# Chunk states stored chunk by chunk and advanced by one step per chunk; silu of two gates taken later, in place

## The chip, the cores and the metric

The kernel runs on one core of a Trainium2 chip. The metric is the device time of one execution in microseconds (us); lower is better. The kernel before has a median of 1754.92 us over 3 runs (1752.55 to 1758.75).

## The reference, cut to what matters

The program is two layers of a hybrid network over 512 latent and 256 context positions of width 1024, followed by a second block (window attention, a gated delta rule, cross-attention and a feed-forward part), which the change does not touch. Each of the first two layers has four branches (short convolution, attention, a gated recurrence called HGRN, a Fourier mix). Each branch is multiplied by `silu` of a gate projection. The recurrence, for 4 heads of width 64 and in both directions d:

```python
def step(state, inp):                       # one chunk of positions
    qc, kc, vc, lf = inp
    a = jnp.cumsum(lf, axis=2)
    a_last = a[:, :, -1:, :]
    s_new = jnp.exp(a_last)[:, :, 0, :, None] * state + jnp.einsum(
        "bhsk,bhsv->bhkv", kc * jnp.exp(a_last - a), vc)
    inter = jnp.einsum("bhtk,bhkv->bhtv", qc * jnp.exp(a), state)
    ...
    return s_new, inter + intra
```

The context chunks come first, then the latent chunks start from the context's last state. `mix_stream` and `hybrid_layer` give the gates: `silu(az)` multiplies the attention output, `silu(hz)` the HGRN output, `silu(cz)` the convolution, `silu(fz)` the Fourier mix.

## The kernel before, in words

Activations lie transposed (channels on the 128 partitions, positions along the free axis), each fp32 matrix is held as a rounded high part and a low part, and every product of the large projections is three matmuls (`mm3`, L187 to L191). Weights come by DMA into `raw`, and `split` (L193) makes the high part `wh` on ScalarE (L194) and the low part `wl` on VectorE or GpSimd (L195).

A layer (`layer`, L547) runs `hgrn` first, then attention with the Fourier and convolution work, then the output projection. `hgrn` (L737) does two rounds, j = 0 and 1, each for two of the four heads (two heads of 64 channels fill 128 partitions). A round computes the decay gates of both directions (Sigmoid, L753 and L754, then Ln, L783), in round 0 also the queries (Silu, L772) and the values `ivt`, and then drives the generator `hgrn_pair` (L807), with projections of gate columns put between its steps:

- round 0: `gate(y[4:6])` (HGRN gates) stands ahead of the pair; `gate(y[2:4])` (attention gates) follows the pair's first step; `gate(y[6:8])` (Fourier gates) follows the second.
- round 1: `gate(y[0:2])` (convolution gates) follows the first step.

`gate` (L993) runs two column blocks of the projection and evicts each from PSUM with a Silu at L998: 128x512 for the latent and, in layer 0 only, 128x256 for the context. `y[2]`, `y[3]`, `y[6]` and `y[7]` are read again only in the attention stage (L1112, L1174).

`hgrn_pair` makes four parts (`hgrn_part`, L834), in the order forward context, forward latent, backward context, backward latent. Chunks are 32 positions: 8 context chunks, 16 latent chunks, 24 states for each direction. A part's first half makes the decayed keys and queries with Exp on ScalarE (L853 to L887) and multiplications on VectorE. Its second half transposes the keys on TensorE (L894), evicts them (`KT`, L896), multiplies keys by values for each chunk (L906, into one double PSUM bank `sc` and two banks `sm`), and evicts these products to the state tile `S` with three copies on ScalarE: L912 for the first two chunks of each 128 positions, and L914 twice for the third and the fourth. The scores (L923) take the same two `sm` banks again, so each of the two score banks needs its L914 to be over. In layer 1 the context parts make no scores. Then VectorE masks and sums the scores (L931 to L939).

The state tile is `S[128, 64, 24]`: value column first, chunk innermost, so that neighbouring value columns of one chunk are 96 bytes apart. After each latent part `hgrn_scan` (L941) makes the recurrence over 24 chunks for all 64 columns with one instruction on VectorE, after spreading the 24 decays to a tile `de` of 1536 columns:

```python
nc.vector.memset(dec[:, 0:1], 0.0)
nc.vector.tensor_copy(de, dec[:, None, :].to_broadcast([128, 64, 24]))
nc.vector.tensor_tensor_scan(S2, de..., S2, 0.0, ALU.mult, ALU.add)
```

`hgrn_out` (L950) then accumulates the outputs: L976 multiplies scores by values (32x64 operands) and queries by the state before each chunk (64x64 operand, `Ss[d][..., :, c - 1]`, read with the 96 byte step). ScalarE squares the sums (L983), and L832 multiplies the normalized result into `y[4 + j]`.

Program order is not engine order. The framework that builds the program plans each engine's order ahead of time: it starts what its own estimate says is ready, the earlier in the program first where several are. Each engine then runs its queue strictly in that planned order, and waits on semaphores. Table loads of ScalarE stand in the queue wherever the next function needs another table than the last.

Of the kernel before, what the change touches and what calls it, by code (L numbers as in the profile page):

```python
# [9 lines left out]
F32 = mybir.dt.float32  # L10
# [3 lines left out]
AF = mybir.ActivationFunctionType  # L14
ALU = mybir.AluOpType
# [5 lines left out]
S = 512  # L21
CTX = 256
T = S + CTX
# [124 lines left out]
class K:  # L148
# [588 lines left out]
    def hgrn(self, l, w_in, need, hp):  # L737
        nc = self.nc
        segs = ((0, 512), (512, 256))
        nt = 6 if need else 4  # L740
        self.hgmask = hp.tile([128, 192], I32, tag="hgmask", name="hgmask", bufs=1)
        nc.scalar.dma_start(self.hgmask, self.I["c_hgmask"])
        self.scanmask = hp.tile([128, 512], F32, tag="scanmask", name="scanmask", bufs=1)
        nc.scalar.dma_start(self.scanmask, self.I["c_scanmask"])
        ivt = hp.tile([128, 6, 256], F32, tag="ivt", name="ivt", bufs=1)
        qs = [None, None]
        for j in range(2):
            u = self.first if l == j == 0 else self.units.take()
            kk = [hp.tile([128, T], F32, tag="kk", name="kk") for _ in range(2)]
            lf = [hp.tile([128, T], F32, tag="lf", name="lf") for _ in range(2)]  # L750

            def evac(d, p, c0, n):
                nc.scalar.activation(kk[d][:, c0:c0 + n], p, AF.Sigmoid, scale=-1.0)  # L753
                nc.scalar.activation(lf[d][:, c0:c0 + n], p, AF.Sigmoid)  # L754

            for d in range(2):
                evac(d, self.cp_gemm(u[d], need_lat=False, tag=("mm" if j else "sm"))[1], 512, 256)
            if j == 0:
                ps = self.lat_gemm(u, ("mm", "mm"))
                self.units.more()  # L760
                for d, p in enumerate(ps):
                    evac(d, p, 0, 512)
            else:
                for d in range(2):
                    evac(d, self.cp_gemm(u[d], need_ctx=False, more=d == 1)[0], 0, 512)
            self.fill()
            if j == 0:
                u = self.units.take()
                for jj in range(2):
                    pl, pc = self.cp_gemm(u[jj], need_ctx=need, more=jj == 1)  # L770
                    q = hp.tile([128, T], F32, tag="q", name="q")
                    nc.scalar.activation(q[:, 0:512], pl, AF.Silu)  # L772
                    if need:
                        nc.scalar.activation(q[:, 512:768], pc, AF.Silu)
                    qs[jj] = q
                self.fill()
                for i, ps in self.tp_panel():
                    nc.scalar.activation(ivt[:, i, :], ps, AF.Copy)
                    if i in (1, 4):
                        self.fill()  # L780
            for d in range(2):
                sc_, bi = self.lscale[:, l, d, j:j + 1], self.lbias[:, l, d, j:j + 1]
                nc.scalar.activation(lf[d], lf[d], AF.Ln, scale=sc_, bias=bi)  # L783
                if l:
                    nc.vector.tensor_scalar(kk[d], kk[d], sc_, None, ALU.mult)
            self.dbg(f"lf{l}{j}0", lf[0]); self.dbg(f"lf{l}{j}1", lf[1])
            if j == 0:
                self.gate(self.y[4:6], need)
            steps = self.hgrn_pair(l, j, kk, lf, qs[j], ivt, need, nt, hp)
            next(steps)  # L790
            if j == 0:
                self.gate(self.y[2:4], need)
                next(steps)
                self.gate(self.y[6:8], need)
                next(steps, None)
            else:
                self.gate(self.y[0:2], need)
                next(steps)
                u = self.units.take()
                for jj in range(2):  # L800
                    for p, (c0, n) in zip(self.cp_gemm(u[jj], need_ctx=need, more=jj == 1), self.segs(need)):
                        ys = self.y[jj][:, c0:c0 + n]
                        nc.vector.tensor_tensor(ys, ys, p, ALU.mult)
                self.fill()
                next(steps, None)

    def hgrn_pair(self, l, j, kk, lf, q, ivt, need, nt, hp):  # L807

        nc = self.nc
        sc = hp.tile([128, 6, 2, 32], F32, tag="sc", name="sc", bufs=1)  # L810
        Ss = [hp.tile([128, 64, 24], F32, tag="S", name="S") for _ in range(2)]
        decs = [hp.tile([128, 24], F32, tag="dec", name="dec") for _ in range(2)]
        parts = [self.hgrn_part(d, c0, n, kk[d], lf[d], q, ivt, need or c0 == 0, j, Ss[d], decs[d], sc, hp)
                 for d in range(2) for c0, n in ((512, 256), (0, 512))]

        next(parts[0])
        for n in range(4):
            if n < 3:
                next(parts[n + 1])
            next(parts[n], None)  # L820
            if n % 2:
                self.hgrn_scan(Ss[n // 2], decs[n // 2], hp)
        yield
        on = self.hgrn_out(lf, Ss, sc, ivt, nt, j, hp)
        yield
        y = self.y[4 + j]
        for (i0, n) in ((0, 4), (4, 2))[:2 if need else 1]:
            tr = self.psum("tr", [128, 128 * n])
            for ii in range(n):
                nc.tensor.transpose(tr[:, 128 * ii:128 * ii + 128], on[:, i0 + ii].rearrange("p h v -> p (h v)"), self.ident)  # L830
            ys = y[:, 128 * i0:128 * (i0 + n)]
            nc.vector.scalar_tensor_tensor(ys, tr, self.col[:, 40 + 2 * l + j:41 + 2 * l + j], ys, ALU.mult, ALU.mult)  # L832

    def hgrn_part(self, d, c0, n, kk, lf, q, ivt, out, j, St, dec, sc, hp):  # L834

        nc = self.nc
        sl = slice(c0, c0 + n)
        nch = n // 32
        ntile = n // 128
        a = hp.tile([128, 512], F32, tag="a", name="a", bufs=1)[:, :n]  # L840
# [8 lines left out]
        o0 = 0 if c0 else 8  # L849
# [51 lines left out]
        for ii in range(ntile):  # L901
            i = c0 // 128 + ii
            for A in range(4):
                rs = slice(32 * A, 32 * A + 32)
                for p in range(2):
                    nc.tensor.matmul(ups[A][64 * p:64 * p + 64, ii], KT[rs, 128 * ii + 64 * p:128 * ii + 64 * p + 64],  # L906
                                     ivt[rs, i, 128 * j + 64 * p:128 * j + 64 * p + 64], start=True, stop=True)
        sv = St[:, :, o0:o0 + nch]
        if d:
            sv = sv[:, :, ::-1]  # L910
        sv = sv.rearrange("p v (i a) -> p a i v", a=4)
        nc.scalar.activation(sv[:, 0:2], u2[:, :, :64 * ntile].rearrange("p a (i v) -> p a i v", v=64), AF.Copy)  # L912
        for A in (2, 3):
            nc.scalar.activation(sv[:, A], ups[A], AF.Copy)  # L914
# [23 lines left out]
                nc.vector.tensor_reduce(s1, M.rearrange("p i (l t) -> p i t l", l=3), AX.X, ALU.add)  # L938
                nc.vector.tensor_tensor(so, so, s1, ALU.add)  # L939

    def hgrn_scan(self, St, dec, hp):  # L941

        nc = self.nc
        nc.vector.memset(dec[:, 0:1], 0.0)
        de = hp.tile([128, 64, 24], F32, tag="de", name="de", bufs=1)
        nc.vector.tensor_copy(de, dec[:, None, :].to_broadcast([128, 64, 24]))
        S2 = St.rearrange("p v c -> p (v c)")
        nc.vector.tensor_tensor_scan(S2, de.rearrange("p v c -> p (v c)"), S2, 0.0, ALU.mult, ALU.add)

    def hgrn_out(self, Qas, Ss, sc, ivt, nt, j, hp):  # L950

        nc = self.nc
        o = self.psum("sc", [128, 2, 512])
        for i in range(nt):
            todo = {}
            for A in range(4):
                qsl = slice(32 * A, 32 * A + 32)
                for p in range(2):
                    t = [(sc[qsl, i, p, :], ivt[qsl, i, 128 * j + 64 * p:128 * j + 64 * p + 64])]
                    for d in range(2):  # L960
                        if i >= 4:
                            c = 4 * (i - 4) + A
                            c = c if d == 0 else 7 - c
                        else:
                            c = 4 * i + A
                            c = 8 + (c if d == 0 else 15 - c)
                        if c == 0:
                            continue
                        x0 = 128 * i + 32 * A
                        t.append((Qas[d][64 * p:64 * p + 64, x0:x0 + 32], Ss[d][64 * p:64 * p + 64, :, c - 1]))  # L970
                    todo[A, p] = t

            for n_ in range(3):
                for (A, p), t in todo.items():
                    if n_ < len(t):
                        nc.tensor.matmul(o[32 * A:32 * A + 32, p, 64 * i:64 * i + 64], *t[n_], start=(n_ == 0), stop=(n_ == len(t) - 1))  # L976
# [13 lines left out]
    def segs(self, need):  # L990
        return ((0, 512), (512, 256)) if need else ((0, 512),)

    def gate(self, tiles, need):  # L993

        u = self.units.take()
        for j in range(2):
            for p, (c0, n) in zip(self.cp_gemm(u[j], need_ctx=need, more=j == 1), self.segs(need)):
                self.nc.scalar.activation(tiles[j][:, c0:c0 + n], p, AF.Silu)  # L998
        self.fill()

    def attention(self, l, w_in, need, ap):
# [1087 lines left out]
```

## Time and profile before

| | |
|---|---|
| median of 3 runs | 1754.92 us (1752.55 to 1758.75) |
| the profiled execution | 1756.17 us, of which its span is 1754.4 us |
| TensorE matmul busy | 1630.6 us, 93% of the span |
| VectorE busy | 1017.9 us, 58% |
| ScalarE busy | 872.1 us, 50% |
| GpSimd busy | 220.4 us, 13% |
| mean granted TensorE clock | 0.965 of 2.4 GHz |

PE is TensorE's matmul side, PEld its weight load, DVE is VectorE, ACT is ScalarE, POOL is GpSimd. A name such as `S<-sc` is the tile written and the tile read. "L914" is a line of the kernel. An entry in square brackets at the end of a timeline row is how long the engine stood idle ahead of it, and what ended that idle time. Some 30 such rows stand below.

### The profile page before, as it was taken

The page shows a single profiled execution, that of the slowest core. Times are in us where ns is not written, and L with a number is a line of the kernel's source. Part 1 is how long each engine was busy: PE and PEld are TensorE (multiplying, and loading weights), DVE is VectorE, ACT ScalarE, POOL GpSimd, SP SyncE. Part 2 cuts the span into 40 slices and gives each one's busy share as a digit, 9 for nine tenths or more (in the row PEclk, how much of TensorE's full clock was granted, in tenths as well). Part 3 has the DMA queues.
Part 4 walks back from the last instruction along what each step waited for, and adds up shares of the span by engine and source line. Part 5 has one row for each costly group of instructions (what it writes and reads, how often), then busy time and mean ns, then how long its engine had stood idle before and what let it go on. Part 6 is the DMA issues. An engine that isn't in the chain of part 4 may idle for free. (4 is left out here: it accounts for less than half of the span.)

```text
span 1754.4 us, 31468 instructions
## 1 busy us (share of the span) xinstructions
PE 1630.6 (93%) x12731; PEld 1334.6 (76%) x12731; DVE 1017.9 (58%) x2133; ACT 872.1 (50%) x1754; POOL 220.4 (13%) x226
## 2 busy tenths in 40 slices
PE   5998979999999887999999889999999999999998
PEld 3876758877778675879787668777788888888886
DVE  4635473676565546586777896778766633333223
ACT  4844662553467474455556732666555533333222
POOL 2100001101230000110213443002100011111000
PEclk8998989999999898999999997999999999999999
DMA  9231203202454111213764234102724533332431
GB/s 361 104 122 51 96 27 130 98 1 67 166 161 168 51 49 56 96 49 96 265 208 135 73 90 97 37 25 70 230 85 168 181 88 99 99 99 85 156 109 72
DMA packets 162574, 193.86 MB, mean 111 GB/s; under 512 B 15054, under 2 KB 124910, under 8 KB 160252
## 3 DMA queue, kind: packets, MB, share of 16 engines
q1 hardware_dynamic: 156604, 183.37, 32.2%
q10 hardware_dynamic: 5824, 8.47, 1.7%
q8 instruction: 100, 1.64, 0.4%
q14 instruction: 46, 0.38, 0.1%
HBM read 175.28 MB, written 13.66 MB: 108 GB/s over the span
## 5 line engine op out<-in xcount | busy, mean ns | idle before, releaser
L194 ACT ACTIVATE wh<-raw 128x512 fp32r<-128x512 f32 (+1 forms) x458 | 282.3, 628 | 435.6 <-PE mm L190 161.2
L195 DVE TENSOR_TENSOR wl<-raw,wh 128x512 fp32r<-128x512 f32 x416 | 285.1, 699 | 357.7 <-ACT wh L194 344.7
L189 PE MATMUL mm<-xh,wh 128*128 128x512 f32 x520 | 208.4, 401 | 1.4 <-ACT acc L1627 1.0
L191 PE MATMUL mm<-xh,wl 128*128 128x512 f32 x520 | 208.1, 401 | 0.0
L190 PE MATMUL mm<-xl,wh 128*128 128x512 f32 x520 | 207.8, 400 | 0.0
L191 PE MATMUL gl<-xh,wl 128*128 128x512 f32 (+1 forms) x480 | 182.4, 381 | 6.0 <-DVE wl L195 3.9
L189 PE MATMUL gl<-xh,wh 128*128 128x512 f32 (+1 forms) x480 | 181.7, 379 | 3.5 <-ACT y L998 2.5
L190 PE MATMUL gl<-xl,wh 128*128 128x512 f32 (+1 forms) x480 | 180.6, 377 | 0.1
L189 PEld LDWEIGHTS mm<-xh,wh 128*128 128x128 f32 x520 | 100.6, 193 | 23.0 <-ACT acc L1627 1.9
L191 PEld LDWEIGHTS mm<-xh,wl 128*128 128x128 f32 x520 | 100.4, 193 | 20.5
L190 PEld LDWEIGHTS mm<-xl,wh 128*128 128x128 f32 x520 | 100.3, 193 | 20.5
L189 PEld LDWEIGHTS gl<-xh,wh 128*128 128x128 f32 x480 | 93.4, 195 | 22.8 <-issue 3.4
L191 PEld LDWEIGHTS gl<-xh,wl 128*128 128x128 f32 x480 | 93.9, 196 | 19.6 <-DVE wl L195 5.2
L190 PEld LDWEIGHTS gl<-xl,wh 128*128 128x128 f32 x480 | 93.5, 195 | 14.3 <-issue 1.1
L195 POOL TENSOR_TENSOR wl<-raw,wh 128x512 fp32r<-128x512 f32 x42 | 58.1, 1388 | 110.8 <-ACT wh L194 74.4
L189 PE MATMUL gc<-ch,wh 128*128 128x256 f32 x224 | 66.6, 299 | 2.6 <-ACT ch L194 2.6
L190 PE MATMUL gc<-cl,wh 128*128 128x256 f32 x224 | 66.5, 297 | 1.8 <-DVE cl L195 1.8
L190 PE MATMUL wo<-wl,yh 128*128 128x512 f32 x160 | 65.0, 407 | 3.1 <-DVE wl L195 2.9
L191 PE MATMUL gc<-ch,wl 128*128 128x256 f32 x224 | 65.8, 294 | 0.0
L191 PE MATMUL wo<-wh,yl 128*128 128x512 f32 x160 | 63.5, 399 | 0.0
L189 PE MATMUL wo<-wh,yh 128*128 128x512 f32 x160 | 63.3, 401 | 0.0
L2005 POOL TENSOR_TENSOR al<-t,ah 128x512 fp32r<-128x512 f32 x22 | 28.3, 1287 | 212.6 <-ACT ah L2004 212.6
(599 smaller groups left out, 3833.4 us busy)
## 6 DMA issues: line engine op xcount, KB each, us to landing
raw<-in_w_in SPq DMA_DIRECT2D x32, 1024.0 KB, 4.9
raw<-in_w_gate_up SPq DMA_DIRECT2D x44, 512.0 KB, 4.8
raw<-in_w_mod SPq DMA_DIRECT2D x16, 1024.0 KB, 6.5
raw<-in_w_out SPq DMA_DIRECT2D x12, 1024.0 KB, 5.4
raw<-in_w_down SPq DMA_DIRECT2D x10, 1024.0 KB, 4.9
mraw<-in_w_mod SPq DMA_DIRECT2D x8, 1024.0 KB, 12.0
raw<-in_w_out SPq DMA_DIRECT2D x16, 512.0 KB, 6.6
raw<-in_w_ckv SPq DMA_DIRECT2D x8, 1024.0 KB, 5.1
```

The lines of the kernel that those rows point to most:

```text
L189: mm(out, ah, bh, start=start, stop=False)
L190: mm(out, ah, bl, start=False, stop=False)
L191: mm(out, al, bh, start=False, stop=stop)
L194: self.nc.scalar.activation(hi, src, AF.Copy)
L195: (eng or self.nc.vector).tensor_tensor(lo, src, hi.bitcast(F32), ALU.subtract)
L2005: nc.gpsimd.tensor_tensor(al[j], t, ah[j].bitcast(F32), ALU.subtract)
```

## The change

The state tile becomes `S[128, 24, 64]`: chunk first, its 64 value columns side by side. The evictions L912 and L914 keep their number, sizes and sources and write runs of 64 neighbouring elements. The memset, the spread of decays and the scan of each direction are replaced by 23 instructions on VectorE, one for each chunk after the first, each on 128x64 and each reading the result of the one before it. The state operand of L976 becomes 64 neighbouring elements. The gates `y[2:4]` and `y[6:8]` are evicted with Copy in place of Silu, and four in-place Silu instructions (128x768 in layer 0, 128x512 in layer 1) stand in the program behind `gate(y[0:2])` of round 1.

```diff
             if j == 0:
-                self.gate(self.y[2:4], need)
+
+                self.gate(self.y[2:4], need, AF.Copy)
                 next(steps)
-                self.gate(self.y[6:8], need)
+                self.gate(self.y[6:8], need, AF.Copy)
                 next(steps, None)
             else:
                 self.gate(self.y[0:2], need)
+                for t in self.y[2:4] + self.y[6:8]:
+                    t = t[:, :T if need else S]
+                    nc.scalar.activation(t, t, AF.Silu)
                 next(steps)
...
-        Ss = [hp.tile([128, 64, 24], F32, tag="S", name="S") for _ in range(2)]
+        Ss = [hp.tile([128, 24, 64], F32, tag="S", name="S") for _ in range(2)]
...
-                self.hgrn_scan(Ss[n // 2], decs[n // 2], hp)
+                self.hgrn_scan(Ss[n // 2], decs[n // 2])
...
-        sv = St[:, :, o0:o0 + nch]
+        sv = St[:, o0:o0 + nch]
         if d:
-            sv = sv[:, :, ::-1]
-        sv = sv.rearrange("p v (i a) -> p a i v", a=4)
+            sv = sv[:, ::-1]
+        sv = sv.rearrange("p (i a) v -> p a i v", a=4)
...
-    def hgrn_scan(self, St, dec, hp):
-
-        nc = self.nc
-        nc.vector.memset(dec[:, 0:1], 0.0)
-        de = hp.tile([128, 64, 24], F32, tag="de", name="de", bufs=1)
-        nc.vector.tensor_copy(de, dec[:, None, :].to_broadcast([128, 64, 24]))
-        S2 = St.rearrange("p v c -> p (v c)")
-        nc.vector.tensor_tensor_scan(S2, de.rearrange("p v c -> p (v c)"), S2, 0.0, ALU.mult, ALU.add)
+    def hgrn_scan(self, St, dec):
+
+        nc = self.nc
+        for c in range(1, 24):
+            nc.vector.scalar_tensor_tensor(St[:, c], St[:, c - 1], dec[:, c:c + 1], St[:, c], ALU.mult, ALU.add)
...
-                        t.append((Qas[d][64 * p:64 * p + 64, x0:x0 + 32], Ss[d][64 * p:64 * p + 64, :, c - 1]))
+                        t.append((Qas[d][64 * p:64 * p + 64, x0:x0 + 32], Ss[d][64 * p:64 * p + 64, c - 1]))
...
-    def gate(self, tiles, need):
+    def gate(self, tiles, need, f=AF.Silu):
...
-                self.nc.scalar.activation(tiles[j][:, c0:c0 + n], p, AF.Silu)
+                self.nc.scalar.activation(tiles[j][:, c0:c0 + n], p, f)
```

## Rows read from the trace of the kernel before

**Rows 1.** The page, part 1: busy time and share of the span of each engine.
```profile
PE 1630.6 (93%) x12731; PEld 1334.6 (76%) x12731; DVE 1017.9 (58%) x2133; ACT 872.1 (50%) x1754; POOL 220.4 (13%) x226
```
**Rows 2.** Stretches (us) of the four rounds: engines' busy time, then PEclk, DMA share, GB/s.
```profile
118.00:177.00 59.00, 50.17 (x1199) 38.01 (x1196) 31.95 (x58) 28.34 (x48) 1.33 (x1) 0.86 0.22 74
204.00:276.00 72.00, 58.93 (x1245) 44.38 (x1245) 48.59 (x96) 46.33 (x81) 1.21 (x1) 0.88 0.18 61
575.00:618.00 43.00, 35.26 (x824) 26.26 (x823) 24.65 (x40) 20.62 (x39) 2.03 (x2) 0.88 0.17 52
640.00:696.00 56.00, 41.88 (x885) 31.37 (x884) 36.28 (x61) 35.33 (x60) 1.01 (x1) 0.85 0.12 39
```
**Rows 3.** Waits, whole span: who waited for whom; us in total, times, longest.
```profile
PE sm L923 <- ACT S L914: 14.5, 18, 2.8
```
**Rows 4.** Timeline of ACT, layer 0, round 0: start, us, instruction, idle before.
```profile
129.22 1.42 ACT L912 ACTIVATE S<-sc 128x512 f32<-128x512 f32 x1
130.35 1.55 ACT L914 ACTIVATE S<-sm 128x256 f32<-128x256 f32 x2
131.92 1.28 ACT L998 ACT_TABLE_LOAD   x1
133.22 0.60 ACT L998 ACTIVATE y<-gl 128x512 f32<-128x512 f32 x1
...
141.44 1.28 ACT L887 ACT_TABLE_LOAD   x1
...
173.71 0.49 ACT L983 ACTIVATE big<-sc 128x384 f32<-128x384 f32 x1 [16.81 <-PE sc L976]
```
**Rows 5.** Timeline of PE, layer 0, round 0.
```profile
131.32 0.33 PE L923 MATMUL sm<-F 64*32 64x32 f32 x16 [2.82 <-ACT S L914]
...
143.68 0.28 PE L906 MATMUL sc<-ivt,KT 32*64 32x64 f32 x4 [1.30 <-ACT KT L896]
...
155.63 0.33 PE L923 MATMUL sm<-F 64*32 64x32 f32 x16 [1.20 <-ACT S L914]
...
167.06 0.84 PE L976 MATMUL sc<-S,lf 64*32 64x64 f32 x32
167.83 0.45 PE L976 MATMUL sc<-ivt,sc 32*32 32x64 f32 x16
```
**Rows 6.** Groups by line and shape, ACT: copies out of PSUM; busy us, mean ns.
```profile
L914 ACT ACTIVATE S<-sm 128x256 f32<-128x256 f32 x16 | 12.4, 921 | 0.0
L912 ACT ACTIVATE S<-sc 128x512 f32<-128x512 f32 x8 | 11.4, 1428 | 5.1 <-PE sm L906 5.1
...
L896 ACT ACTIVATE KT<-tr 128x512 f32<-128x512 f32 x8 | 5.1, 638 | 2.7 <-DVE s L938 1.4 <-DVE sc L935 1.3
...
L1007 ACT ACTIVATE kv<-tp 128x256 f32<-128x256 f32 x12 | 4.6, 382 | 23.1 <-PE tp L191 23.1
```
**Rows 7.** Groups by line and shape, DVE.
```profile
L948 DVE TENSOR_TENSOR_SCAN S<-de,S 128x1536 f32<-128x1536 f32 x8 | 26.9, 3358 | 22.8 <-ACT S L914 22.8
...
L946 DVE COPY de<-dec 128x1536 f32<-128x1536 f32 x8 | 7.6, 951 | 2.3 <-ACT dec L853 2.2
...
L1833 DVE SCALAR_TENSOR_TENSOR S<-S,gl,sm 128x128 f32<-128x128 f32 x16 | 5.4, 341 | 1.9 <-PE sm L1831 1.3 <-PE mm L1825 0.5
...
L939 DVE TENSOR_TENSOR sc<-sc,s 128x64 f32<-128x64 f32 x4 | 0.9, 224 | 0.1
```
**Rows 8.** Timeline of DVE, layer 0, round 0.
```profile
147.68 0.37 DVE L938 TENSOR_REDUCE s<-M 128x64 f32<-128x192 f32 x1
148.09 0.22 DVE L939 TENSOR_TENSOR sc<-sc,s 128x64 f32<-128x64 f32 x1
...
156.24 3.36 DVE L948 TENSOR_TENSOR_SCAN S<-de,S 128x1536 f32<-128x1536 f32 x1 [4.09 <-ACT S L914]
```
**Rows 9.** Timeline of ACT around the start of layer 1's attention.
```profile
695.93 0.63 ACT L194 ACTIVATE yh<-y 128x512 fp32r<-128x512 f32 x1
...
699.56 0.39 ACT L1007 ACTIVATE kv<-tp 128x256 f32<-128x256 f32 x1 [3.00 <-PE tp L191]
```

## Prediction

> **What bounds the kernel now.** I read the page first: TensorE's matmul side is busy for 93% of the span and no other engine comes near it [rows 1], so time is won only where TensorE stands idle or runs at the lower of its two clock levels (1.2 against 2.4 GHz). Next I cut out the four rounds of the recurrence, the stretches that the change touches [rows 2]. They take 230 us, and TensorE is busy for 186 of them. The idle time is 8.8, 13.1, 7.7 and 14.1 us, 43.8 in all. The granted clock there is 0.85 to 0.88, against 0.965 over the whole run. Length times missing clock gives 8.3, 8.6, 5.2 and 8.4 us, 30.5 in all, as the most that a full clock could give back in these stretches. The wait table then says who ends the idle time: the largest share that the change can reach is the score matmuls' wait for the state evictions, 14.5 us in 18 waits, the longest 2.8 [rows 3]. The two timelines of layer 0's first round show how it comes about: the products L906 are done, ScalarE copies them to `S` in a row of three [rows 4], and the scores need the two `sm` banks that the last two of these copies release [rows 5].
>
> **The evictions, part by part.** L912 takes 1428 ns for 128x512 and each L914 921 ns for 128x256. ScalarE's other copies out of PSUM of the same sizes, into neighbouring elements, take 638 and 382 ns [rows 6]. L914 reads one PSUM bank in order, as L1007 does; what differs is the 96 byte step on the writing side. The change takes that step away, so I give L912 and L914 the prices of L896 and L1007. From the start of L912 to the end of the first L914, when the first score bank is free, it now takes 2.1 us: the start is at 129.22, the two L914 end at 131.90 after some 0.6 us between one end and the next, and the waiting matmul goes at 131.32 [rows 4, 5]. It becomes 0.6 + 0.4, and with the overlap that the rows show between neighbouring copies about 0.9. That is 1.2 us off the first wait of each of the eight latent parts, and the second wait, of about 0.3, goes too. A wait of 1.20 us such as the second one shown in [rows 5] vanishes; the one of 2.82 keeps 1.6, since there the copies also start late, behind other work in ScalarE's queue. Context parts have half the columns and short waits. Of the 14.5 us [rows 3] about 2.6 stay: **11.9 us gained**. The bounds are 0 (the cause is on the reading side) and 14.5.
>
> **The gates.** In the first round of layer 0 the gate evictions fall among the Exps of ScalarE: a table load of 1283 ns, then a Silu, then a load back. Four loads of this round, the first at 131.92 and the last at 141.44 [rows 4], are not needed with Copy. The switch costs 1.30 us by the start times of load and Silu, 131.92 and 133.22 [rows 4], so 5.2 us of ScalarE. What of it TensorE sees is one wait: the eviction of the keys, queued behind two such loads, holds L906 back by 1.30 us [rows 5]. **1.3 us gained**, bounds 0 and 5.2. The Trainium skill, "ScalarE: Activation LUTs", section "What ACT_TABLE_LOAD costs", prices a switch at about 2.66 us, since a drain follows the load; by that the four would free 10.6 us. The trace disagrees: the Silu starts 1.30 us after the load does [rows 4].
>
> The four in-place Silus per layer are new. A 128x512 costs about 0.64 us, a 128x768 about 0.9 (638 ns, and 256 ns more for each 256 columns, [rows 6]): four times each, 6.2 us of ScalarE. Where they run is the planner's matter. Program order puts them in the second round, but the planner starts what is ready: the split of `y` for the output projection, which the program has behind the whole attention, runs at 695.93, ahead of the attention's first `kv` at 699.56 [rows 9]. So I expect the Silus soon after their gates, in ScalarE's idle times, of which the 16.81 us ahead of L983 is the first [rows 4]. There they are covered. Without this cover, one per layer stands ahead of a state eviction and shifts it by its load and its own length, 1.3 + 0.6 to 0.9; about half of that reaches TensorE. **I charge 2.0 us**, bounds 0 and 13 (the second rival).
>
> **The steps.** Removed for each direction: scan 3.36 us, spread 0.95, and a memset. Added: 23 instructions of 128x64. No row is the same operation; it lies between L939, 128x64 without the per-partition scalar, 224 ns, and L1833, the same operation with such a scalar on 128x128, 341 ns [rows 7]. I take 0.28, the middle. Each needs the one before it: in [rows 8] L939 depends on L938 and starts 0.41 us after it, 0.04 behind its end. So 0.32 us a step, 7.4 for 23, bounds 5.2 (23 x 0.224) and 8.8 (23 x 0.38). In place of 4.3 us VectorE works 5 to 9, at most 36 us more over the eight directions, on an engine that is busy for 141 of the 230 us [rows 2]. On the path to the outputs stands the scan alone, 3.36 against 7.4, less the 1.5 us by which the copies end earlier: the states come 2.5 us later. The first matmul that reads the backward states starts at 167.06 [rows 5], the scan ends at 159.60 [rows 8]: 7.5 us of slack, filled on TensorE by gate projections. Forward states have a whole part more. On the other side small steps let VectorE's other work in between, where the scan holds the queue for 3.36 us. **I charge nothing**, bounds 0 and 10 (2.5 us in each of four rounds). What is late next is the masked sums that L976 also reads.
>
> The Trainium skill, "VectorE: DVE Perf Modes", section "Rules for kernel authors" and its words on the drain, speaks against this part: it advises to minimize the count of operations, because each one waits for the pipe to empty. Rows and page agree on the direction; whether it reaches the end of the kernel is the third rival.
>
> **The operand of L976.** 32 matmul records with the strided states take 0.84 us, 16 with neighbouring values 0.45 [rows 5]: 26 and 28 ns each. Nothing gained; bounds 0 and 6, if each 0.84 us (six in this round, fewer in layer 1) fell by a third in every round. The Trainium skill, "SBUF — State Buffer", section "Door 1: The DMA port swizzle", says that each access that crosses to another 16 byte line pays a penalty; by that these matmuls would get faster. Equal pace in the trace says they do not.
>
> **The clock.** The waits removed, 13.2 us, are 30% of the 43.8 us idle [rows 2]. If lost clock goes with idle time, 30% of 30.5 us, 9 us, comes back; if the stretches of lower clock only move, nothing does. Half is **4.5 us**.
>
> **Sum.** Against the profiled execution, 1756.17 us (span 1754.4): 11.9 + 1.3 + 4.5 - 2.0 = 15.7 gained, so 1740.5 us. That is 14.4 below the median of 1754.92. The profiled run stands 1.3 above that median; a measurement of this kernel can tell about 0.3%, 5.3 us, from no change.
>
> **Rivals.**
> *The clock comes back more fully* (same mechanism, larger): the rounds lie in short idle gaps, and with the scores no longer waiting the clock may stay up. If half of the 30.5 us of lost clock comes back, 15.2, with 13.2 of waits and no charge, the time is 1728. For it speaks that four clock figures of 0.85 to 0.88 go with the four rounds [rows 2]; against it, that 2.6 us of these waits and 29 us of other idle time stay. Chance 0.18. Faster L976 would give 1734.5, chance 0.04.
>
> *The Silus fall among Exps.* The gate that the program puts them behind is itself evicted among Exps. A misplaced Silu costs two switches and itself, 2 x 1.30 + 0.64 to 0.9, 3.4 us; eight of them 27 us of ScalarE. Half on the path, 13 us, gives 1753.5, no change; with four misplaced 1747. For it: ScalarE is busy for 46 of 72 us in the second round [rows 2]. Against: the planner's early start in [rows 9]. Chance 0.12, half of it within 0.3%.
>
> *The steps take the scan's place as the wait* (the other side). If a step costs 0.38 or more and the planner sets all 23 in one row ahead of the masked sums, VectorE's queue is late by 8.8 - 3.4 = 5.4 us in each of eight directions, 43 us. What follows in that queue is the next part's factors and the weight halves `wl`, for which TensorE waits. It decides from the point where more than 15.7 of these 43 us reach TensorE; at two thirds, 29 us, the time is 1769. Against it: the slack of 7.5 us and the choice that the planner has among ready work. Chance 0.07.
>
> *The change does not do what it says:* the copies stay at 1.4 and 0.9 us because the layout was not their cause. Then 1.3 gained and 2.0 charged: 1757, no change. Against it stand the equal sizes in [rows 6]. Chance 0.04.
>
> **How the numbers follow.** The forecast's own case has 0.55 and reaches from 1735 to 1747. Faster than 0.3% below the median: 0.55 + 0.18 + 0.04 and half of 0.12, 0.83. Same: the other half and 0.04, 0.10. Slower: 0.07. The range reaches down to the full clock, 1728, and up to 1752, which takes in most of the misplaced Silus.
>
> **What would show it.** Right: L912 near 0.64 and L914 near 0.38 us; the score wait for L914 at about 3 us in place of 14.5; four table loads fewer in layer 0's first round; 184 steps of 0.22 to 0.34 us; L976 at the same pace; clock in the rounds at 0.88 to 0.91. Wrong: copies as long as before, Silus with a load on either side, TensorE waiting for a step or for `wl` behind the steps, or the same idle time under another name, such as the first part's keys.

## The result, and the profile after

The changed kernel has a median of 1728.08 us (1726.01 to 1733.74, 4 runs) beside 1756.84 us of the kernel before on the same chip: the ratio is 0.9839, 95% interval 0.982 to 0.9857, or 28 us less. On another chip, later, it was 0.9824 (0.9801 to 0.9847). The forecast had the direction and, narrowly, the range (1728 to 1752); the likeliest value, 1740.5, was 12 us too high. The time came out at the value that the first rival gave, though only in part for that rival's reason.

The first view is the page's busy time of each engine, after the change; it answers to [rows 1]. TensorE is 21.5 us less busy, while it computes the same products.

```profile
PE 1609.1 (93%) x12731; PEld 1320.7 (77%) x12731; DVE 1025.1 (59%) x2293; ACT 858.0 (50%) x1760; POOL 220.6 (13%) x226
```

To see where the time went I cut both traces at the same instructions: the first key transposes of a round, the first `kv` eviction of each attention, and the first Sigmoid load of layer 1. The first three columns are start and end, length, and PE busy; PEclk stands after POOL. First before, then after.

```profile
118.30:207.60 89.30, 79.89 (x1383) 63.05 (x1379) 40.88 (x75) 43.04 (x74) 2.66 (x2) 0.90 0.21 73
207.60:285.62 78.02, 65.53 (x1300) 51.17 (x1301) 52.96 (x112) 46.11 (x79) 3.70 (x5) 0.89 0.20 67
519.90:638.87 118.97, 110.50 (x1326) 90.24 (x1324) 58.68 (x97) 69.54 (x116) 2.55 (x3) 0.96 0.28 93
638.87:699.56 60.69, 45.23 (x904) 34.17 (x905) 38.99 (x66) 37.01 (x61) 2.49 (x4) 0.86 0.14 44
```
```profile
117.47:199.38 81.91, 75.35 (x1382) 60.14 (x1379) 44.00 (x118) 38.94 (x76) 2.67 (x2) 0.94 0.23 79
199.38:269.82 70.44, 61.59 (x1300) 49.26 (x1301) 53.62 (x152) 41.56 (x80) 3.43 (x5) 0.93 0.22 75
506.71:620.66 113.95, 106.84 (x1326) 88.34 (x1324) 59.99 (x137) 67.67 (x120) 2.55 (x3) 0.99 0.29 97
620.66:672.84 52.18, 42.26 (x904) 32.02 (x905) 41.56 (x111) 33.20 (x62) 3.47 (x5) 0.87 0.19 60
```

The four stretches are 347.0 us before and 318.5 after: these 28.5 us are the whole gain, and the rest of the kernel takes 1407.4 us before and 1407.6 after. TensorE's idle time (length less PE busy) falls from 45.8 to 32.4, by 13.4 us. Its busy time falls by 15.1. Of that the state matmuls of the outputs give 6.8: 16.8 us busy before, 10.0 after, in the groups by line and shape below. The other 8.3 are a difference: the same matmuls, at a higher granted clock (0.94, 0.93, 0.99 and 0.87 in place of 0.90, 0.89, 0.96 and 0.86). Length times missing clock falls from 30.8 to 17.8 us.

The groups by line and shape of the kernel after: TensorE's state matmuls, ScalarE's state copies ([rows 6] before), its in-place Silus, and the steps on VectorE.

```profile
L977 PE MATMUL sc<-S,lf 64*32 64x64 f32 x624 | 10.0, 227 | 1.2 <-issue 1.2
```
```profile
L918 ACT ACTIVATE S<-sm 128x256 f32<-128x256 f32 x16 | 5.2, 385 | 0.0
L916 ACT ACTIVATE S<-sc 128x512 f32<-128x512 f32 x8 | 4.7, 588 | 3.3 <-PE sm L910 3.3
...
L801 ACT ACTIVATE y<-y 128x768 f32<-128x768 f32 x4 | 3.4, 847 | 0.1
```
```profile
L949 DVE SCALAR_TENSOR_TENSOR S<-S,dec 128x64 f32<-128x64 f32 x184 | 50.2, 280 | 9.1 <-ACT S L918 5.4 <-ACT S L916 0.3
```

The copies went from 1428 and 921 ns to 588 and 385, near the prices that copies into neighbouring elements had before [rows 6]. The wait table of the kernel after ([rows 3] before) shows what this did to the scores' wait, and which waits of TensorE are left:

```profile
PE tr L898 <- DVE kt L861: 10.6, 8, 3.2
...
PE sc L910 <- ACT KT L900: 4.7, 5, 1.4
PE sm L927 <- ACT S L918: 4.1, 5, 1.7
```

ScalarE's timeline of layer 0's first round after ([rows 4] before). The row of three copies runs from 128.52 to 129.65 where it took 2.7 us. The in-place Silus stand in the program behind `gate(y[0:2])` of the second round, whose first eviction starts at 213.32, but the first of them runs 75 us ahead of that. The second one and its load stand right ahead of a row of state copies:

```profile
128.52 0.58 ACT L916 ACTIVATE S<-sc 128x512 f32<-128x512 f32 x1
129.00 0.65 ACT L918 ACTIVATE S<-sm 128x256 f32<-128x256 f32 x2
129.53 0.61 ACT L999 ACTIVATE y<-gl 128x512 f32<-128x512 f32 x1
...
136.63 1.28 ACT L801 ACT_TABLE_LOAD   x1
137.93 0.85 ACT L801 ACTIVATE y<-y 128x768 f32<-128x768 f32 x1
138.79 1.28 ACT L873 ACT_TABLE_LOAD   x1
...
147.51 1.28 ACT L801 ACT_TABLE_LOAD   x1
148.81 0.85 ACT L801 ACTIVATE y<-y 128x768 f32<-128x768 f32 x1
149.56 0.58 ACT L916 ACTIVATE S<-sc 128x512 f32<-128x512 f32 x1
```

TensorE then waits for this row, and in layer 1 for another one behind a Silu (the load is at 575.96, the Silu at 577.25, L916 at 577.79):

```profile
150.46 0.59 PE L927 MATMUL sm<-F 64*32 64x32 f32 x28 [0.89 <-ACT S L918]
...
578.70 0.33 PE L927 MATMUL sm<-F 64*32 64x32 f32 x16 [0.90 <-ACT S L918]
```

TensorE's timeline at the outputs of the same round ([rows 5] before): 32 records with the state operand now take 0.38 us from start to next start (162.16 to 162.54), as long as 16 records with `ivt`.

```profile
162.16 0.46 PE L977 MATMUL sc<-S,lf 64*32 64x64 f32 x32
162.54 0.45 PE L977 MATMUL sc<-ivt,sc 32*32 32x64 f32 x16
162.92 0.46 PE L977 MATMUL sc<-S,lf 64*32 64x64 f32 x32
```

### The profile page after: what moved, and what is told of

Read it like the earlier page. It is cut to its first block, busy times and chain, and to the rows that moved or that the text cites. A ratio compares the mean times of both kernels' runs of the same rounds, so it can differ in the third digit from the quotient of the medians.

```text
span 1726.1 us, 31635 instructions
## 1 busy us (share of the span) xinstructions
PE 1609.1 (93%) x12731; PEld 1320.7 (77%) x12731; DVE 1025.1 (59%) x2293; ACT 858.0 (50%) x1760; POOL 220.6 (13%) x226
## 4 chain that ended last, share of the span: by engine, by line
PE 66%; DVE 18%; ACT 7%; issue 5%; DMA 2%; POOL 2%; ACTq 0%; DVEq 0%; POOLq 0%; SPq 0%
PE mm L190 7%; PE mm L189 7%; PE mm L191 7%; PE gl L189 4%; PE gl L190 4%; PE gl L191 4%; DVE acc L1630 2%; DVE wl L195 2%; PE tr L1110 2%; PE gc L191 1%; PE gc L190 1%; PE gc L189 1%; PE tr L1100 1%; PE rg L190 1%; PE wo L190 1%
## 5 line engine op out<-in xcount | busy, mean ns | idle before, releaser
L949 DVE SCALAR_TENSOR_TENSOR S<-S,dec 128x64 f32<-128x64 f32 x184 | 50.2, 280 | 9.1 <-ACT S L918 5.4
```

The lines of the kernel that those rows point to most:

```text
L949: nc.vector.scalar_tensor_tensor(St[:, c], St[:, c - 1], dec[:, c:c + 1], St[:, c], ALU.mult, ALU.add)
```

## The experiments

Three theories stood after the result. A: the layout carries the gain, by shorter evictions, a state operand that streams at a higher pace, and the clock, taken to follow them. B: the gates do, by table loads taken out of the runs of Exp. C: the fine steps do, since the scan held VectorE's queue for 3.4 us at a time. Ratios are to the kernel before on the same chip; 0.1% is 1.76 us.

**The gates alone.** The kernel before with the gate part of the diff and nothing else.

> The kernel before with the gate part of the change alone. Theory A (the shorter evictions, the faster state operand and the clock that follows them carry the gain): nearly nothing, 0 to 3 us faster than before, since two table switches fewer meet TensorE in one wait of 1.3 us. Theory B (the gain is mostly the table loads taken out of the runs of Exp): 8 us or more faster.

Ratio 0.9992 (0.9974 to 1.0011): no change, and B falls. TensorE still waits 14.4 us for the copies, at the lines this kernel has them on:

```profile
PE sm L926 <- ACT S L917: 14.4, 16, 2.8
...
PE gl L191 <- DVE wl L195: 4.5, 2, 3.2
```

**The states alone.** Layout and steps, gates as before.

> The kernel before with the state layout and the steps, gates as before. Theory A: 24 to 29 us faster than before, nearly the whole gain; score waits for L914's line near 4 us in place of 14.5, state matmul records at 12 ns in place of 26. Theory B: less than 18 us faster.

Ratio 0.9853 (0.9826 to 0.988), about 26 us faster: the whole gain within the intervals. The state matmuls are 10.1 us busy, and the score wait is 2.3 us:

```profile
PE sm L923 <- ACT S L914: 2.3, 3, 1.7
```

**The steps alone, on the old layout.**

```diff
-        nc.vector.memset(dec[:, 0:1], 0.0)
...
-        nc.vector.tensor_tensor_scan(S2, de.rearrange("p v c -> p (v c)"), S2, 0.0, ALU.mult, ALU.add)
+        for c in range(1, 24):
+            nc.vector.scalar_tensor_tensor(St[:, :, c], St[:, :, c - 1], dec[:, c:c + 1], St[:, :, c], ALU.mult, ALU.add)
```

> The kernel before with 23 steps in place of the scan, but on the old layout (96 byte step between neighbouring elements), gates as before. Theory A: the copies keep 1.43 and 0.92 us, so no gain: within 3 us of before. Theory C (the fine steps let the other VectorE work through, where the scan blocked its queue for 3.4 us, and that is what shortened the rounds): 8 us or more faster. If the steps are a burden that the layout's gain covers: 3 us or more slower.

Ratio 0.999 (0.9974 to 1.0005). So C falls as the main cause. The score wait is as before, 15.8 us. With the 96 byte step an instruction takes 375 ns in place of 280:

```profile
L945 DVE SCALAR_TENSOR_TENSOR S<-S,dec 128x64 f32<-128x64 f32 x184 | 68.2, 375 | 12.4 <-ACT S L914 6.0 <-ACT S L912 2.7
```

Even these long steps cost no more than the scan did. One thing of C is true: TensorE's two waits for weight halves queued on VectorE (3.9 us in the kernel before, 4.5 in the gates-only run above) are gone here and in the changed kernel. In five of the later runs with steps one of them is back, with 0.8 to 1.4 us.

**Which half of the layout?** In two runs the steps write a second tile `So`, so that copies and operand can have different layouts. A third has both in the new layout and is their control.

```diff
+        So = hp.tile([128, 64, 24], F32, tag="So", name="So")
+        nc.vector.tensor_copy(So[:, :, 0], St[:, 0])
         for c in range(1, 24):
-            nc.vector.scalar_tensor_tensor(St[:, c], St[:, c - 1], dec[:, c:c + 1], St[:, c], ALU.mult, ALU.add)
+            nc.vector.scalar_tensor_tensor(So[:, :, c], So[:, :, c - 1], dec[:, c:c + 1], St[:, c], ALU.mult, ALU.add)
+        return So
```

> The changed kernel, but the steps write into a second tile in the old layout, so that the evictions stay short and only the state operand of the output matmuls has the 96 byte step again (one 128x64 copy more for each direction). Theory A: 5 to 8 us slower than the changed kernel (1733 to 1737), the state matmul records back at 24 to 26 ns. Rival (the operand's layout is hidden, as forecast): within 2 us of the changed kernel.

> The changed kernel, but the evictions write the old layout and the steps carry the states into a second tile in the new one, so that only the copies are long again. Theory A: 12 to 22 us slower than the changed kernel (1740 to 1750), score waits for the copies back at 12 to 15 us and the clock of the four rounds back near 0.87. Rival (the copies are not what matters): within 4 us of the changed kernel.

> The changed kernel, but the steps write into a second tile of the same, new layout (one 128x64 copy more for each direction): the control for the two runs with a second tile, with copies and operand both in neighbouring elements. If a second tile costs nothing by itself: within 2 us of the changed kernel. If it costs (VectorE's extra copy, other buffer waits, another plan): 3 to 8 us slower, which is then to be taken off what those two runs showed.

The control is at 0.9833 (0.9803 to 0.9863), no slower than the changed kernel beside it (0.9824): the second tile is free. The strided operand gives 0.9923 (0.9904 to 0.9942), 16 us worse than the control, and the strided evictions 0.9959 (0.9944 to 0.9974), 22 us worse (the control ran on another chip; by the intervals each difference is known to some 6 us). The first loses about twice what A expected, the second the most that it expected. Both also have long steps, since in each of them one of the two tiles has the 96 byte step (two tensor operands of every step in the first run, one in the second): 184 steps take 68 us of VectorE in place of 52. The groups of the three runs, strided operand, strided evictions, control:

```profile
L980 PE MATMUL sc<-So,lf 64*32 64x64 f32 x624 | 17.3, 343 | 2.0 <-issue 2.0
```
```profile
L951 DVE SCALAR_TENSOR_TENSOR So<-So,dec,S 128x64 f32<-128x64 f32 x184 | 68.2, 372 | 5.0 <-ACT S L918 1.5
```
```profile
L918 ACT ACTIVATE S<-sm 128x256 f32<-128x256 f32 x16 | 12.4, 921 | 0.0
L916 ACT ACTIVATE S<-sc 128x512 f32<-128x512 f32 x8 | 11.4, 1428 | 4.7 <-PE sm L910 4.7
```
```profile
L980 PE MATMUL sc<-So,lf 64*32 64x64 f32 x624 | 9.6, 222 | 3.2 <-issue 3.2
```
```profile
PE sm L927 <- ACT S L918: 14.3, 18, 2.2
```
```profile
L980 PE MATMUL sc<-So,lf 64*32 64x64 f32 x624 | 10.2, 227 | 4.7 <-issue 4.7
```
```profile
L951 DVE SCALAR_TENSOR_TENSOR So<-So,dec,S 128x64 f32<-128x64 f32 x184 | 51.6, 282 | 5.7 <-ACT S L918 2.1
```

So each side of the layout has its own effect, in the profile as in the time: with the strided operand the state matmuls are 7.1 us longer and the score wait stays short, at 1.5 us; with strided copies the matmuls stay fast and the wait is back at 14.3 us, where the control has 1.8.

The granted clock did not go the way that A expected. Below are the four rounds of the strided-evictions run and then of the control, cut as above:

```profile
118.28:201.06 82.78, 72.76 (x1383) 58.99 (x1379) 47.38 (x120) 41.22 (x74) 2.67 (x2) 0.98 0.22 78
201.06:275.62 74.56, 61.32 (x1300) 49.01 (x1301) 58.21 (x154) 45.98 (x80) 3.71 (x5) 0.91 0.21 70
510.92:627.73 116.81, 107.68 (x1325) 88.41 (x1324) 64.72 (x139) 72.19 (x120) 2.55 (x3) 0.97 0.28 95
627.73:686.47 58.74, 43.07 (x904) 32.88 (x905) 46.30 (x113) 37.69 (x63) 3.48 (x5) 0.88 0.17 53
```
```profile
118.61:200.90 82.29, 74.37 (x1382) 60.16 (x1379) 43.10 (x120) 36.81 (x74) 2.66 (x2) 0.96 0.22 79
200.90:269.35 68.45, 58.68 (x1300) 47.44 (x1301) 53.77 (x154) 41.54 (x80) 3.71 (x5) 0.98 0.22 76
506.19:619.16 112.97, 107.34 (x1326) 88.25 (x1324) 60.67 (x139) 67.82 (x120) 2.54 (x3) 0.98 0.29 98
619.16:673.32 54.16, 43.96 (x904) 33.56 (x905) 41.95 (x113) 33.27 (x62) 3.47 (x5) 0.84 0.18 57
```

With the long copies the rounds are 15.0 us longer, and 14.5 of these are idle time, 48.1 us against 33.5. The score wait alone makes 12.5 of it. TensorE's busy time is the same within 0.5 us, and length times missing clock is 18.9 us against 15.6, far from the 30.8 of the kernel before, though the idle time is above the 45.8 it had there. So the evictions cost the wait, and the clock that the changed kernel won does not hang on that wait.

**What a longer recurrence costs.** Each step is followed by a copy back, so that the chain has twice as many instructions.

```diff
-            nc.vector.scalar_tensor_tensor(St[:, c], St[:, c - 1], dec[:, c:c + 1], St[:, c], ALU.mult, ALU.add)
+            nc.vector.scalar_tensor_tensor(So[:, c], St[:, c - 1], dec[:, c:c + 1], St[:, c], ALU.mult, ALU.add)
+            nc.vector.tensor_copy(St[:, c], So[:, c])
```

> The changed kernel with the recurrence made about twice as long on VectorE: each step writes a second tile and a 128x64 copy brings the result back, 184 copies more, 43 us or more of VectorE. If the steps are covered, as forecast: within 3 us of the changed kernel. If the steps are on TensorE's path (the third rival of the prediction): 10 us or more slower, mostly in the rounds, and about 0.4 us for each us that the slow steps of the runs with a 96 byte step add.

Ratio 0.9908 (0.9881 to 0.9934), 15 us slower than the changed kernel beside it (0.9824, 0.9801 to 0.9847) for 33.7 us more of VectorE: 0.44 us each. The cover of the steps is thin. The first two rounds are 8.7 us longer than in the changed kernel on the same chip; 2.8 of that are idle time, and 5.9 are as many of TensorE's matmuls at a lower granted clock (0.94 and 0.89 against 0.98 and 0.93). VectorE is busy for 60 of 77 us in the second round, and a wait that was 1.0 us in the changed kernel becomes the third longest of TensorE, the output transposes for VectorE's normalized result:

```profile
PE tr L834 <- DVE big L989: 6.3, 3, 2.7
```
```profile
200.71:277.48 76.77, 65.41 (x1300) 51.20 (x1301) 60.31 (x198) 39.79 (x79) 4.33 (x5) 0.89 0.26 90
```

At this rate the longer steps of the two strided runs (16.6 us more of VectorE) stand for about 7 us. By this estimate some 9 us are left for the operand and some 15 for the evictions; with the 2 us of the steps-alone run and the 7 by which the 280 ns steps beat the 375 ns ones that is 33, against the 26 to 31 measured for the layout with its steps. The rate is taken from one run and need not hold in the others.

**Longer copies without longer steps.** The changed kernel with each state copy issued twice.

> The changed kernel with each eviction of the states issued twice in a row (the second writes the same values again), so that ScalarE needs about 2.2 us for a latent part's row in place of 1.1, near the 2.7 of the strided copies, while steps and operand stay as fast as they are. If the length of the evictions carries what the strided-eviction run lost beyond its slower steps (about 16 us): 8 to 14 us slower than the changed kernel (1735 to 1742), score waits back at 8 to 12 us. If that run was slow mostly because its steps took 0.37 us: less than 5 us slower.

Ratio 0.9888 (0.984 to 0.9936), median 1734.62: some 9 us slower by the ratio, 6.5 by the medians, with a wide interval. The direction is as expected, but the score wait is only 4.3 us, in 10 waits, where the changed kernel has 4.1: the planner put repeated copies behind the first ones of another bank, so the first score bank came free as soon after the row's start as without them. Its profile does not show where the time went: the four rounds together take 319.8 us, 1.3 more than in the changed kernel. It does not settle the evictions' share. The better figure is the 12.5 us of score wait in the strided-evictions run above.

**More gates by Copy.** In three runs the convolution gates of the second round, and in one of them all gates, are evicted by Copy; the last of the three keeps Silu for the attention and Fourier gates.

```diff
-                self.gate(self.y[0:2], need)
-                for t in self.y[2:4] + self.y[6:8]:
+                self.gate(self.y[0:2], need, AF.Copy)
+                for t in self.y[0:2] + self.y[2:4] + self.y[6:8]:
```

> The changed kernel, with the convolution gates of the second round evicted by Copy as well and their Silu in the same row as the other four. It takes away the loads on either side of four Silus among the Exps of the second rounds. If ScalarE still sets the pace there: 2 to 6 us faster than the changed kernel (1722 to 1726). If the planner only puts the in-place Silus among the Exps instead: the same within 2 us.

> As the run before it, and the HGRN gates of the first round evicted by Copy too, with their Silu in place ahead of the attention gates in the program. It takes the load of Exp at the head of the first round's keys away (1.3 us ahead of the first key multiplication in each layer). If that head is on TensorE's path: 1 to 3 us faster than the run before it; if not, the same within 2 us.

> State layout and steps of the changed kernel; attention and Fourier gates evicted with Silu as in the kernel before; convolution gates of the second round evicted with Copy and made Silu in place. If the last round's gain seen with these gates (52.2 to 46.6 us) holds and the first round keeps the time it has without in-place Silus: 2 to 6 us faster than the changed kernel. If the gates only shift where the clock falls: the same within 3 us.

> The changed kernel as it is, beside the three others on one chip: 1726 to 1731, so that the others are compared with it on the same chip.

Ratios 0.9852 (0.9833 to 0.9872), 0.9851 (0.9824 to 0.9878) and 0.9825 (0.9798 to 0.9851), beside 0.9839 and 0.9824 for the changed kernel (the last of the three and the 0.9824 are from one chip). None beats it. The last round of the first of them, cut at the first `kv` eviction, is 46.61 us, 5.6 less than the 52.18 of the changed kernel; this is the 46.6 of the third expectation. The cut misleads here. That eviction has moved ahead of the round's last work: 901 of TensorE's and 102 of VectorE's instructions lie ahead of it, where the changed kernel has 904 and 111. At the fourth `kv` eviction the counts agree. First this run, then the changed kernel:

```profile
622.17:679.81 57.64, 48.58 (x976) 39.66 (x977) 40.78 (x111) 33.38 (x66) 4.09 (x5) 0.97 0.24 84
```
```profile
620.66:681.48 60.82, 50.90 (x976) 40.66 (x977) 41.56 (x111) 34.36 (x65) 3.79 (x5) 0.89 0.24 80
```

So 3.2 us are won there, 2.3 of them in busy time, and the total does not follow. Behind the first `kv` eviction all the profiles have 1053 to 1059 us, and two profiles of the changed kernel itself differ there by 4.3, so a few us in one profile decide nothing.

## Why the prediction was right, and where it was off

- *The evictions, 11.9 us.* Right in mechanism and size. L916 and L918 took 588 and 385 ns where 638 and 382 were forecast. The score wait went from 14.5 to 2.3 us in the states-only run, 12.2 gained, and to 4.1 in the changed kernel, where the Silus take 1.8 back (next point). The wait of 2.82, of which 1.6 was to stay, kept 1.73. The bounds of 0 and the "does not do what it says" rival fell.
- *The gates, 1.3 gained and 2.0 charged.* The charge was right, the gain was not. In each layer one in-place Silu stands with its load ahead of a row of state copies, and the scores wait 0.89 and 0.90 us for that row; in the states-only run, which has no in-place Silus, neither of the two waits is there. That is 1.8 us, by the mechanism that the charge named. The wait of 1.30 us for the keys that was to go did go, but others came, and the keys' wait as a whole is 4.6 us before and 4.7 after. In layer 0's first round two loads fewer are left rather than four, since the first in-place Silu stands among the Exps with a load on either side, 136.63 and 138.79. That is the second rival, once out of eight. The other five Silus run in ScalarE's idle times, as forecast. The gates-only run's "no change" fits the sum of -0.7, but cannot tell it from 0.
- *The operand of L976, 0.* This is the step that failed most. It compared the strided state records (64x64) with the `ivt` records (32x64) and took an equal pace per record for an equal price. Contiguous state records run at 12 ns, half of 26, and 6.8 us came from that. A likely reason why the `ivt` records misled lies in the kernel's operands: for one position block the `ivt` records of both heads use the same 32 rows of the array, while the state records use two groups of 64 rows. No run tests this reason. Nearer for a comparison were the score matmuls, on tiles of the same 64x32 shape: in the trace before, 48 of them start from 156.96 to 157.36, 8 ns for 32 columns each. The Trainium skill, "SBUF — State Buffer", section "Door 1: The DMA port swizzle", says that each access that crosses to a new 16 byte line pays a penalty. The prediction set that rule aside; the runs with either operand layout agree with its direction, at 17.3 against 10.2 us busy.
- *The clock, 4.5 of 9.* Undersized, and its premise did not hold. TensorE's busy time without the state matmuls fell by 8.3 us; the missing clock fell by 13.0, or 42%, where the idle time fell by 29%, the share that the prediction used. By its own measure the first rival was nearly right in size, 13.0 against 15.2. But "if lost clock goes with idle time" is what the strided-evictions run contradicts: in its profile the idle time is back, at 48.1 us, and the clock is not lost again. The steps alone have 26.2 us of missing clock with 43.7 us idle, so they may bring a part. What raised the clock stays open.
- *The steps, 0.* They took 280 ns where 0.28 was the middle of the bounds, and steps on the old layout cost no more than the scan. But "charged nothing" named a cover that is thin: 33.7 us more of VectorE cost 15. The slower rival's mechanism is real; the change stays below the point from which it decides. The Trainium skill, "VectorE: DVE Perf Modes", section "Rules for kernel authors", advises few operations. Here 23 in place of three cost nothing, 46 did.

Side by side, for the four rounds: the waits had 11.9 + 1.3 - 2.0 = 11.2 us and gave 13.4 (10.4 of score wait, 3.9 of waits for weight halves that the forecast did not have, the rest 0.9 the other way); the operand had 0 and gave 6.8; the clock had 4.5 and gave 8.3. That is 15.7 forecast and 28.5 measured. So the evictions were understood and the direction followed from them. That the time still fell into the range, at its edge, is luck in part: 6.8 us came from a term put at nothing, and the 1728 of the first rival was met with the operand's help.

## What to carry to other kernels

Store a tile in the order in which its writers and its matmuls walk through it, even if one long instruction over the other order has to become a chain of short ones, as long as the engine that runs the chain has room. When two matmul groups are compared to price a layout, take groups that occupy the array in the same way: an equal pace of groups that are placed differently did not show an equal price here. And when the order on an engine is planned by a program, the place of an instruction in the source says little about where it runs; read it from the trace.

## What the runs showed that was not expected

- A step of 96 bytes between elements slowed each of the three engines that met it, by different factors: ScalarE's 128x512 copy took 1428 ns in place of 588, a 128x64 step on VectorE about 372 in place of 280 whether one, two or all three of its tensor operands had it, and TensorE's 64-row moving operand 26 ns a record in place of 12.
- The granted clock did not follow the idle time. The four rounds have 30.8 us of missing clock with 45.8 us idle before, and 18.9 with 48.1 in the strided-evictions run.
- A scan of 3.36 us on VectorE seems to have had a second price, two waits of TensorE for weight halves that stand behind it in VectorE's queue. No view names these as the scan's. In the runs with steps both are gone, or one is left with at most 1.4 us.
